# A convolution group ahead of the first head: which unit of work opens a kernel that TensorE bounds

## The chip, the cores and the metric

The kernel runs on one core of one Trainium2 chip. The metric is the device time of one execution in microseconds (us), where less is better. Three runs of the kernel before gave 903.43, 903.62 and 904.82 us; the median is 903.62. The chip's engines are named as follows: TensorE (PE in the profile) multiplies matrices and writes to PSUM; VectorE (DVE), ScalarE (ACT) and GpSimd (POOL) work element by element; SyncE (SP) issues the transfers.

## The reference

The reference computes one layer of a hybrid decoder on 2048 rows of 1024 columns, with 16 learned meta rows in front. All is float32. Cut to what matters:

```
hn = rms_norm(h, norm_g)                      # h: 16 meta rows, then x
proj = hn @ w_in                              # 1024 -> 8 * 512
cx, cb, cc, cg, q, k, v, rg = split(proj, 8)

conv_out = cb * conv3(cc * cx) * silu(cg)     # causal, 3 taps, per channel
q, k = rotary(q) * d**-0.5, rotary(k)         # 4 heads of 128
ret = group_norm(retention(q, k, v))          # chunks of 128 rows, a state per head
ret_out = ret * silu(rg)

h = h + concat(conv_out, ret_out) @ w_out
out = rms_norm(h, final_g)[16:]
```

The 512 channels of the convolution are four groups of 128, and the retention has four heads of 128. A group needs the four projections cc, cx, cg and cb; a head needs k, v, q and rg.

## The kernel before, in words

**Rounds and units.** The rows are worked in two rounds (`r`) of 1024 rows, each in two halves (`j`) of 512. A round consists of eight units: heads 0 to 3, then convolution groups 0 to 3. A last stage multiplies with `w_out`, pair by pair of row blocks.

**Quads.** Each unit has two quads. A quad multiplies two projections (`i`) by the two halves `j` of the round. A head's first quad gives K and V, its second Q and RG; a group's first gives CC and CX, its second CG and CB. For accuracy each float32 operand is split into a high and a low part (`split`, L99 on ScalarE for the cast and L111, or L103, on VectorE for the rest), and a product of blocks takes three matmuls for each of four slices of 128, so 12 matmuls of 128 by 512.

There are two kinds of quad. `quad` (matmuls at L208) needs seven products of blocks instead of eight, at the price of sums of blocks: `stationary` forms four sums of weight blocks on GpSimd (L108 and L111) and splits seven weight blocks, and `m` holds seven splits of x or of sums of its blocks. `quad_plain` (matmuls at L258) takes the blocks as they are, eight products. Round 0 opens with two plain quads, since the sums of x need time; round 1 opens with one, and the last stage with one.

**The opening of round 0.** While x is loaded and split, the two plain quads of the first unit run. Their weights are held in the tiles that later hold splits 2 and 3 of x (`FIRST_W`, `PLAIN_W`), and split 7 of x shares its tile with split 4 (`B12`). So those splits can only be made once a plain quad has passed: block sums are formed by `block_sums` (L172), splits 2 and 6 follow, and splits 3 and 4 are left to the function named `rest`, which is called after the unit's second quad through `between`. The normalisation of x is left out of the products: the factor of each row, `rr`, and its square, `rr2`, are made by `row_factors` (squares on ScalarE at L317, `rsqrt_mean`, and `spread`, which writes a diagonal to the tile `rot`, L281, multiplies it with ones, L288, and copies the result on ScalarE, L291 and L293), and multiplied in afterwards. The tile `rot` has one buffer, and the rotation of K and Q (`rotary`, L512 to L515) uses the same one.

**A head.** `take` copies or sums each result out of PSUM and rotates K and Q; RG is multiplied by `rr` (L556) and goes through Silu (L557). Then the meta rows give the first state (`meta_state`), and for each half K and V are transposed (L573, L578), states are updated (L588, L591), masked scores `pm` are formed (L601, L603) and applied (L611, L612), normalised (L617 to L628), transposed back (L635) and stored (`store_mixed`, L439). This follows the head's quads in program order, so it lies beside the quads of the next unit.

**A group.** In `conv_group` the first quad gives u = CC * CX * rr2. `meta_carry` gives the last two meta columns, `carry` copies them in front of u, `taps` applies the three taps (L452 on ScalarE, L454 twice on VectorE), and the second quad's results are multiplied in (L466, on VectorE and GpSimd).

**Beside the units.** After a unit's second quad `ahead` loads the next unit's raw weight blocks (L431) and, in round 0, multiplies them with the meta rows (`meta_products`, L392); only then may the block sums overwrite the raw blocks. After heads 1 to 3, two steps each of `later` prepare the block sums of the next round's x and of `w_out` in memory. After each group of round 0, three steps of `steps` make the row factors of round 1.

**What sets the order.** The program is written in the order above. A planner places the instructions of each engine from that order and from modelled times, when their inputs and a buffer are free; each engine then runs its own list strictly in order. The transfers all go through SyncE's queue. Buffers are shared by tag: `g` (16 tiles of a half row block, for x, u, K, V and others), `ra` (8 raw blocks), `tc` (4), `b` (2), and 4 banks of PSUM each for projections (`pj`) and for all else (`ms`).

The loop that the change touches:

```
        for h in range(NG):
            blocks = head(h, r, m, rot_t, f, blocks, lambda: ahead(r, h + 1), *((first, between) if h == 0 else ()))
            if h > 0:
                next(later, None)
                next(later, None)
        steps = row_factors(r + 1, factors[r + 1]) if r < NR - 1 else iter(())
        for g in range(NG):
            blocks = conv_group(g, r, m, f, blocks, lambda: ahead(r, NG + g + 1))
            for _ in range(3):
                next(steps, None)
```

Of the kernel before, what the change touches and what calls it, by code (L numbers as in the profile page):

```python
# [11 lines left out]
AF = mybir.ActivationFunctionType  # L12
# [7 lines left out]
NG = 4  # L20
EPS = 1e-6
HB = 512
# [9 lines left out]
BLOCK = ((0, 7), (1, 5))  # L32
FIRST_W, PLAIN_W, B12 = 2, 3, 4
SUMS = (3, 2, 4, 6)


def retention_constants():
# [31 lines left out]
def hybrid_trunk(ctx: ExitStack, tc: tile.TileContext, t, out: bass.AP, chunk_decay):  # L69
# [5 lines left out]
    nc = tc.nc  # L75
# [14 lines left out]
    def gen(name="g"):  # L90
        return sb.tile([P, HB + 16], F32, name=name, tag="g", bufs=GEN)[:, : 2 + HB]
# [21 lines left out]
    def load_raw(loads):  # L113
        tiles = []
        for load in loads:
            a = raw()
            load(a)
            tiles.append(a)
        return tiles

    def stationary(blocks):

        a11, a12, a21, a22 = blocks
        s1 = sb.tile([P, HB], F32, name="sa", tag="ra", bufs=RAW)

        def parts(src):
            hi = sb.tile([P, HB], F32R, name="wh", tag="wh", bufs=RING)
            lo = sb.tile([P, HB], F32R, name="wl", tag="wl", bufs=RING)
            split(hi, lo, src)
            return hi, lo  # L130

        w = [parts(a11), parts(a12)]
        add(nc.gpsimd, s1, a21, a22)
        sub(nc.gpsimd, a21, a11, a21)
        sub(nc.gpsimd, a11, s1, a11)
        sub(nc.gpsimd, a12, a12, a11)
        return w + [parts(a) for a in (a11, s1, a21, a12, a22)]
# [61 lines left out]
    def quad(w, m, take):  # L199


        def product(i, bank, first):
            (wh, wl) = w[i]
            for kt in range(KH):
                ks = slice(kt * P, (kt + 1) * P)
                mh, ml = m[i][kt]
                for n, (a, b) in enumerate(((wl, mh), (wh, ml), (wh, mh))):
                    nc.tensor.matmul(  # L208
                        bank, a[:, ks], b, start=first and kt == 0 and n == 0, stop=kt == KH - 1 and n == 2,
                        skip_group_check=not first,  # L210
                    )

        def copy(bank):
            c = sb.tile([P, HB], F32, name="tc", tag="tc", bufs=COPIES)
            nc.scalar.copy(out=c, in_=bank)  # L215
            return c

        xb = ps_proj()
        product(0, xb, True)
        c = copy(xb)  # L220
        yb = ps_proj()
        product(1, yb, True)
        take(0, 0, yb, c)
        product(2, xb, False)
        u2 = copy(xb)
        zb = ps_proj()
        product(3, zb, True)
        c = copy(zb)
        product(4, xb, False)
        take(1, 1, xb, c)  # L230
        product(5, zb, False)
        take(0, 1, zb, u2)
        product(6, xb, False)
        take(1, 0, xb, None)
# [195 lines left out]
    def w_loads(n):  # L430
        return [lambda a, i=i: nc.sync.dma_start(a, t["w_in"][n, i]) for i in range(4)]  # L431
# [18 lines left out]
    def taps(u, g):  # L450
        c = gen("c")[:, :HB]
        nc.scalar.mul(c, u[:, 2:], conv_w[:, g, 2:3])  # L452
        for tap in (1, 0):
            nc.vector.scalar_tensor_tensor(  # L454
                out=c, in0=u[:, tap : tap + HB], scalar=conv_w[:, g, tap : tap + 1], in1=c, op0=ALU.mult, op1=ALU.add
            )
        return c

    def conv_group(g, r, m, f, blocks, ahead):

        u = [gen("u") for _ in range(2)]
        rr, rr2 = ([a[:, j * HB : (j + 1) * HB] for j in range(2)] for a in f[:2])
        held = [None]

        def mul(eng, out, a, b):
            eng.tensor_tensor(out=out, in0=a, in1=b, op=ALU.mult)  # L466

        def take(i, j, pp, c):
            s = u[j][:, 2:]
            if c is None:  # L470
                mul(nc.vector, s, pp, s)
            elif i == 1:
                add(nc.vector, c, pp, c)
                held[0] = c
            else:
                add(nc.vector, s, pp, c)
                mul(nc.vector, s, s, rr2[j])
                if j == 1:
                    mul(nc.gpsimd, s, s, held[0])

        blocks, meta = blocks
        quad(stationary(blocks), m, take)
        if meta:
            meta_carry(g, meta)
        carry(u, g, r)
        cs = [taps(u[j], g) for j in range(2)]

        def take(i, j, pp, c):
            if i == 0:
                add(nc.vector, c, pp, c)  # L490
                mul(nc.vector, c, c, rr[j])
                nc.scalar.activation(c, c, AF.Silu)  # L492
                mul(nc.gpsimd, cs[j], cs[j], rr[j])
                mul(nc.gpsimd, cs[j], cs[j], c)
                return
            if c is not None:
                add(nc.vector, c, pp, c)
                pp = c
            mul(nc.vector, cs[j], pp, cs[j])

        n = 2 * (NG + g) + 1
        quad(stationary(load_raw(w_loads(n))), m, take)
        blocks = ahead()
        for j in range(2):
            store_mixed(r, j, g, cs[j])
        return blocks
# [205 lines left out]

    def ahead(r, n):

        if n == 2 * NG:
            return None
        blocks = load_raw(w_loads(2 * n))
        return blocks, meta_products(blocks) if r == 0 else None
# [4 lines left out]
    for r in range(NR):  # L723
        f = factors[r]
        rot_t = sb.tile([P, 2, BLK], F32, name="rot_t", tag="rot_t", bufs=1)
        p0 = NMETA + r * BLK

        def load_tables():
            nc.sync.dma_start(rot_t, t["rot"][:, :, p0 : p0 + BLK])

        if r == 0:
            w = [None] * 4
            loads = w_loads(0)

            def begin(half):
                for n in (half, 2 + half):
                    w[n] = plain_part(n, loads[n], FIRST_W)

            m, b = moving(
                load_x(r), gain_of, {(0, 0): lambda: begin(0), (0, KH - 1): lambda: begin(1), (0, KT - 1): normalise_meta}  # L740
            )
            first = [[p for a, p in w]]
            blocks = None, meta_products([a for a, p in w])
            first.append(plain_parts(w_loads(1)))
            load_tables()
            nc.sync.dma_start(cols, t["cols"])
            t3 = [a[:, i * HB : (i + 1) * HB] for a in (row_tile("t3") for _ in range(2)) for i in range(2)]
            t1 = [brief("t1") if n < BRIEF else sb.tile([P, HB], F32, name="t1", tag="tc", bufs=COPIES) for n in range(KH)]
            for kt in range(KH):
                b11, b21, b12, b22 = (b[n * KH + kt] for n in range(4))  # L750
                block_sums(b11, b12, b22, b21, t1[kt], t3[kt], gain_of(kt), gain_of(KH + kt), nc.gpsimd)
                parts(m, 2, kt, b22)
                parts(m, 6, kt, b21)
            for _ in row_factors(0, f):
                pass
            nc.sync.dma_start(causal, t["causal"])
            nc.sync.dma_start(conv_w, t["conv_w"])
            nc.sync.dma_start(ret_g, t["ret_norm_g"])

            def rest():  # L760
                for i, held in ((3, t1), (4, t3)):
                    for kt in range(KH):
                        parts(m, i, kt, held[kt])

            between = (lambda: None, rest)
            later = prepare(load_x(1), sums_x, gain_of)
        else:
            m, b = moving(load_x(r), gain_of)
            first = [plain_parts(w_loads(0))]
            load_tables()  # L770
            prepared(m, sums_x, (1, 3))
            between = (lambda: prepared(m, sums_x, (0, 2)),)
            blocks = None, None
            later = prepare(load_w_out, sums_w)
        for h in range(NG):
            blocks = head(h, r, m, rot_t, f, blocks, lambda: ahead(r, h + 1), *((first, between) if h == 0 else ()))
            if h > 0:
                next(later, None)
                next(later, None)
        steps = row_factors(r + 1, factors[r + 1]) if r < NR - 1 else iter(())  # L780
        for g in range(NG):
            blocks = conv_group(g, r, m, f, blocks, lambda: ahead(r, NG + g + 1))
            for _ in range(3):
                next(steps, None)

    m, b = moving(load_w_out)
    final_g = row_tile("final_g")
# [41 lines left out]
```

## Time and profile before

| | before |
|---|---|
| median of three runs | 903.62 us (903.43 to 904.82) |
| the profiled execution | 903.85 us, span 902.1 us |
| TensorE busy | 885.0 us, 98% of the span |
| VectorE busy | 714.6 us, 79% |
| ScalarE busy | 406.1 us, 45% |
| GpSimd busy | 398.9 us, 44% |
| mean granted clock of TensorE | 0.994 |

The span runs from the first to the last instruction of the profiled execution; 1.75 us of that execution lie around it. A row of a view of groups gives the source line, the engine, the operation, the tiles out<-in with their shapes, the count, then the busy time and the mean duration in ns, and then the idle time in front with what ended it. A row of a timeline gives start and duration in us. A row of windows gives the stretch, its length, the busy time of the engines PE, PEld (weight load), DVE, ACT and POOL with the number of instructions, then the granted clock of TensorE, the share of the transfer engines and GB/s. In a row of the waits, the last three numbers are the total in us, the number of waits and the longest one.

### The profile page before, as it was taken

To read this page: it belongs to the slowest core of one execution; us is meant where nothing else is said; L and a number is where in the kernel's file an instruction comes from. 1 tells how busy PE (TensorE), PEld (TensorE's weight loads), DVE (VectorE), ACT (ScalarE), POOL (GpSimd) and SP (SyncE) were. 2 spreads that over 40 slices of the span, in tenths; PEclk is the share of its full clock that TensorE was granted. 3 is DMA by queue.
4 is the path that set the end of the run, shared out by engine and by line. 5 is a ranking of instruction groups with operands and counts; after the bars stand their busy time and mean duration, and the time that the engine had idled before them with its cause. 6 is when DMAs were issued, how large, how long until landed. Compare 5 with 4: busy or idle time off the path is not lost.

```text
span 902.1 us, 12862 instructions
## 1 busy us (share of the span) xinstructions
PE 885.0 (98%) x4407; PEld 727.8 (81%) x4407; DVE 714.6 (79%) x1173; ACT 406.1 (45%) x815; POOL 398.9 (44%) x294
## 2 busy tenths in 40 slices
PE   8998999999999999999999999999999999999996
PEld 5787888888878777788888888888888878788885
DVE  6798888897686776899889899777667697866764
ACT  8771342424344443655333332433333465554553
POOL 0533132323355554461333323345546445777763
PEclk9998999999999999999999999999999999999999
DMA  9711352623234232744125262113231685555532
GB/s 333 239 40 38 104 195 59 205 82 107 79 103 127 78 108 78 253 180 141 38 73 203 73 236 68 50 56 90 57 88 48 210 280 178 162 186 152 182 111 93
DMA packets 76242, 116.94 MB, mean 130 GB/s; under 512 B 7632, under 2 KB 24336, under 8 KB 76176
## 3 DMA queue, kind: packets, MB, share of 16 engines
q1 hardware_dynamic: 76176, 116.11, 40.1%
q8 instruction: 35, 0.57, 0.3%
q14 instruction: 31, 0.25, 0.1%
HBM read 90.92 MB, written 25.17 MB: 129 GB/s over the span
## 4 chain that ended last, share of the span: by engine, by line
PE 83%; DVE 9%; DMA 3%; ACT 2%; issue 2%; POOL 1%; SPq 0%; POOLq 0%; DVEq 0%; ACTq 0%
PE pj L208 66%; PE pj L258 7%; DVE ml L111 2%; DVE wl L111 2%; PE ms L611 2%; PE ms L612 1%; PE ms L601 1%; PE ms L588 1%; PE ms L392 1%; DVE rot L513 1%; DMA ra<-in_w_in 1%; PE ms L635 1%; PE ms L573 1%; DVE rot L512 1%; PE ms L578 1%
## 5 line engine op out<-in xcount | busy, mean ns | idle before, releaser
L208 PE MATMUL pj<-mh,wl 128*128 128x512 f32 x1008 | 400.0, 397 | 1.0 <-ACT tc L215 0.8
L208 PE MATMUL pj<-ml,wh 128*128 128x512 f32 x1008 | 394.2, 391 | 1.1 <-DVE ml L111 1.1
L208 PE MATMUL pj<-mh,wh 128*128 128x512 f32 x1008 | 393.4, 390 | 0.0
L99 ACT CAST wh<-ra 128x512 fp32r<-128x512 f32 x216 | 133.8, 620 | 315.1 <-PE pj L208 272.4
L208 PEld LDWEIGHTS pj<-mh,wl 128*128 128x128 f32 x1008 | 189.6, 188 | 43.1 <-ACT tc L215 2.2
L208 PEld LDWEIGHTS pj<-ml,wh 128*128 128x128 f32 x1008 | 189.8, 188 | 39.6 <-DVE ml L111 1.9
L208 PEld LDWEIGHTS pj<-mh,wh 128*128 128x128 f32 x1008 | 189.6, 188 | 39.8
L111 DVE TENSOR_TENSOR wl<-ra,wh 128x512 fp32r<-128x512 f32 x216 | 192.4, 892 | 36.2 <-ACT wh L99 35.2
L111 POOL TENSOR_TENSOR ra<-ra 128x512 f32<-128x512 f32 x72 | 113.0, 1570 | 82.0 <-DVE qg L556 32.3
L108 POOL TENSOR_TENSOR sa<-ra 128x512 f32<-128x512 f32 x36 | 54.9, 1525 | 122.6 <-DVE wl L111 62.1
L111 POOL TENSOR_TENSOR ra<-sa,ra 128x512 f32<-128x512 f32 x36 | 52.2, 1450 | 98.3 <-DVE wl L111 98.0
L215 ACT COPY tc<-pj 128x512 f32<-128x512 f32 x108 | 62.6, 580 | 0.0
L258 PE MATMUL pj<-ml,mh 128*128 128x512 f32 x128 | 50.8, 396 | 0.1
L258 PE MATMUL pj<-mh,mh 128*128 128x512 f32 x128 | 50.2, 395 | 0.0
L258 PE MATMUL pj<-mh,ml 128*128 128x512 f32 x128 | 48.5, 396 | 1.5 <-DVE ml L111 1.5
L624 POOL TENSOR_TENSOR rp<-rs,neg_half 128x4 f32<-128x4 f32 x16 | 19.9, 1245 | 51.0 <-DVE rs L108 50.8
L466 POOL TENSOR_TENSOR c<-c,rr 128x512 f32<-128x512 f32 x16 | 30.0, 1874 | 24.0 <-DVE c L454 13.6
L108 DVE TENSOR_TENSOR tc<-pj,tc 128x512 f32<-128x512 f32 x32 | 22.0, 688 | 23.4 <-PE pj L208 23.4
L111 DVE TENSOR_TENSOR ml<-t,mh 128x512 fp32r<-128x512 f32 x40 | 36.6, 961 | 0.8 <-ACT mh L99 0.8
L99 ACT CAST wh<-sa 128x512 fp32r<-128x512 f32 x36 | 22.3, 620 | 32.7 <-PE pj L208 32.7
L665 DVE TENSOR_TENSOR yo<-pj,yo 128x512 f32<-128x512 f32 x32 | 22.0, 688 | 18.8 <-POOL yo L108 8.9
L466 POOL TENSOR_TENSOR c<-c,tc 128x512 f32<-128x512 f32 x16 | 27.3, 1706 | 19.0 <-ACT tc L492 17.6
(128 smaller groups left out, 1134.3 us busy)
## 6 DMA issues: line engine op xcount, KB each, us to landing
ra<-in_w_in SPq DMA_DIRECT2D x128, 256.0 KB, 2.7
x<-in_xT SPq DMA_DIRECT2D x48, 256.0 KB, 5.1
w<-in_w_out SPq DMA_DIRECT2D x32, 256.0 KB, 5.0
ra<-mixed SPq DMA_DIRECT2D x32, 256.0 KB, 2.7
yo<-in_x SPq DMA_DIRECT2D x32, 256.0 KB, 4.4
ra<-in_x SPq DMA_DIRECT2D x16, 256.0 KB, 3.7
mixed<-qg SPq DMA_DIRECT2D x16, 256.0 KB, 2.3
sums_x<-x SPq DMA_DIRECT2D x16, 256.0 KB, 2.4
```

The source lines that it names most:

```text
L99: nc.scalar.copy(out=hi, in_=src)
L108: eng.tensor_tensor(out=out, in0=a, in1=b, op=ALU.add)
L111: eng.tensor_tensor(out=out, in0=a, in1=b, op=ALU.subtract)
L208: nc.tensor.matmul(bank, a[:, ks], b, start=first and kt == 0 and n == 0, stop=kt == KH - 1 and n == 2, skip_group_check=not first,)
L215: nc.scalar.copy(out=c, in_=bank)
L258: nc.tensor.matmul(banks[i], a[:, ks], b, start=half + kt + n == 0, stop=half == 1 and kt == KH - 1 and n == 2,)
L392: nc.tensor.matmul(four[i], meta_s[:, i % 2 * KH + kt, :], blocks[i][:, kt * P : (kt + 1) * P], start=kt == 0, stop=kt == KH - 1,)
L466: eng.tensor_tensor(out=out, in0=a, in1=b, op=ALU.mult)
L512: nc.vector.tensor_tensor(out=rot[:h, :w], in0=a[h:], in1=table[h:, 1, :], op=ALU.mult)
L611: nc.tensor.matmul(o[:, cs], pm[:, cs], vt[j][:, cs], start=True, stop=False)
L624: nc.gpsimd.tensor_tensor(out=rp, in0=rs, in1=neg_half.rearrange("p (c a) -> p c a", a=1), op=ALU.pow)
L665: last[0] = nc.vector.tensor_tensor(out=y, in0=pp, in1=y, op=ALU.add)
```

## The change

The order of the units is written down in a table, and round 0 runs group 0 first, then heads 0 to 3, then groups 1 to 3. Round 1 keeps its order. The two plain quads of round 0 go to group 0: the first weights loaded are those of CC and CX, the next those of CG and CB. `conv_group` gets a plain form of its two quads: in the first, CC is copied out of PSUM by ScalarE and CX multiplied onto it by VectorE, and the products with `rr2` follow when the quad is done; in the second, all four results are copied by ScalarE and multiplied afterwards. Head 0 takes the seven-product quads. Because one group now stands ahead of the heads, the steps that make the row factors of round 1 are taken four at a time after groups 1 to 3.

```
+UNITS = (4, 0, 1, 2, 3, 5, 6, 7), (0, 1, 2, 3, 4, 5, 6, 7)
...
-    def conv_group(g, r, m, f, blocks, ahead):
+    def conv_group(g, r, m, f, blocks, ahead, first=(), between=()):
+        between = iter(between)
...
+        def take_plain(i, j, pp, c):
+            s = u[j][:, 2:]
+            if i == 0:
+                nc.scalar.copy(out=s, in_=pp)
+            else:
+                mul(nc.vector, s, pp, s)
+
         blocks, meta = blocks
-        quad(stationary(blocks), m, take)
+        if len(first) > 0:
+            quad_plain(first[0], m, take_plain)
+        else:
+            quad(stationary(blocks), m, take)
+        next(between, lambda: None)()
+        if len(first) > 0:
+            for j in range(2):
+                mul(nc.vector, u[j][:, 2:], u[j][:, 2:], rr2[j])
         if meta:
             meta_carry(g, meta)
         carry(u, g, r)
         cs = [taps(u[j], g) for j in range(2)]
+
+        def take_plain(i, j, pp, c):
+            c = gen("cb")[:, :HB]
+            nc.scalar.copy(out=c, in_=pp)
+            if i == 0:
+                mul(nc.vector, c, c, rr[j])
+                nc.scalar.activation(c, c, AF.Silu)
+                mul(nc.gpsimd, cs[j], cs[j], rr[j])
+            mul(nc.vector, cs[j], cs[j], c)
...
-        quad(stationary(load_raw(w_loads(n))), m, take)
+        if len(first) > 1:
+            quad_plain(first[1], m, take_plain)
+        else:
+            quad(stationary(load_raw(w_loads(n))), m, take)
+        next(between, lambda: None)()
         blocks = ahead()
...
-            loads = w_loads(0)
+            loads = w_loads(2 * NG)
...
-            first.append(plain_parts(w_loads(1)))
+            first.append(plain_parts(w_loads(2 * NG + 1)))
...
-            def rest():
+            def late_parts():
...
-            between = (lambda: None, rest)
+            between = (lambda: None, late_parts)
...
         steps = row_factors(r + 1, factors[r + 1]) if r < NR - 1 else iter(())
-        for g in range(NG):
-            blocks = conv_group(g, r, m, f, blocks, lambda: ahead(r, NG + g + 1))
-            for _ in range(3):
-                next(steps, None)
+        units = UNITS[r]
+        for n, unit in enumerate(units):
+            following = units[n + 1] if n + 1 < len(units) else None
+            rest = lambda: ahead(r, following)
+            special = (first, between) if n == 0 else ()
+            if unit < NG:
+                blocks = head(unit, r, m, rot_t, f, blocks, rest, *special)
+                if unit > 0:
+                    next(later, None)
+                    next(later, None)
+            else:
+                blocks = conv_group(unit - NG, r, m, f, blocks, rest, *special)
+                if n > 0:
+                    for _ in range(4 - r):
+                        next(steps, None)
```

More of the change, by code (lines that the diff above doesn't have):

```diff
@@ L713, in ahead @@
     def ahead(r, n):
-        if n == 2 * NG:
+        if n is None:
             return None
@@ L774, in hybrid_trunk @@
             later = prepare(load_w_out, sums_w)
[L775 to L779, printed above, removed]
-        steps = row_factors(r + 1, factors[r + 1]) if r < NR - 1 else iter(())
-        for g in range(NG):
-            blocks = conv_group(g, r, m, f, blocks, lambda: ahead(r, NG + g + 1))
-            for _ in range(3):
-                next(steps, None)
+        steps = row_factors(r + 1, factors[r + 1]) if r < NR - 1 else iter(())
+        units = UNITS[r]
[13 more added lines that the diff above has]
+                        next(steps, None)
     m, b = moving(load_w_out)
```

## The prediction

> **What bounds the kernel now.** I read the page first. TensorE is busy for nearly the whole span, so the kernel can only get shorter where TensorE stands still or runs at a lower clock.
>
> ```profile
> span 902.1 us, 12862 instructions
> PE 885.0 (98%) x4407; PEld 727.8 (81%) x4407; DVE 714.6 (79%) x1173; ACT 406.1 (45%) x815; POOL 398.9 (44%) x294
> ```
>
> The waits of TensorE come second. One wait holds most of what can be won: a matmul of a head's retention waits for the masked scores pm, which VectorE writes. The next row shows how small the others are.
>
> ```profile
> PE ms L611 <- DVE pm L603: 3.7, 1, 3.7
> PE pj L208 <- ACT tc L215: 0.8, 2, 0.7
> ```
>
> Third come the windows around it. The last column but two is the granted clock.
>
> ```profile
> 65.00:76.06 11.06, 11.06 (x60) 9.27 (x60) 10.88 (x18) 3.93 (x9) 3.19 (x2) 1.00 0.19 49
> 76.06:79.81 3.75, 0.00 (x1) 0.00 (x1) 3.70 (x8) 0.62 (x1) 0.00 (x0) 0.85 0.25 70
> 79.81:85.52 5.71, 5.71 (x22) 5.23 (x22) 3.47 (x14) 0.00 (x0) 2.01 (x3) 0.50 0.12 46
> 78.60:78.80 0.20, 0.00 (x0) 0.80 0.00 0
> ```
>
> In the hole VectorE is busy for 3.70 of 3.75 us, so VectorE is the bound there. The clock falls to half inside the slice 78.60 to 78.80, some 2.7 us into the hole, and stays there for 5.7 us of work after it. The timeline of TensorE prices this, with two rows of the later chain for the same retention matmuls at full clock.
>
> ```profile
> 75.22 0.39 PE L208 MATMUL pj<-mh,wl 128*128 128x512 f32 x1
> 75.67 0.39 PE L208 MATMUL pj<-mh,wh 128*128 128x512 f32 x1
> 79.81 0.79 PE L611 MATMUL ms<-kv,pm 128*128 128x128 f32 x2 [3.75 <-DVE pm L603]
> 83.24 0.77 PE L208 MATMUL pj<-mh,wl 128*128 128x512 f32 x1
> 85.52 0.42 PE L208 MATMUL pj<-mh,wh 128*128 128x512 f32 x1
> 439.05 0.22 PE ms L611 x2
> 440.83 8.18 PE pj L208 x36
> ```
>
> Sixteen small matmuls took 83.24 - 79.81 = 3.43 us, where the later sixteen took 440.83 - 439.05 = 1.78: 1.65 lost. The five large steps from 83.24 to 85.52 took 2.28 us; at full clock (75.22 to 75.67 is two steps, 0.225 each) they take 1.13: 1.15 lost. Hole and clock together are 3.75 + 2.8 = 6.55, say 6.5 us.
>
> Why is VectorE late there? The chain of waits from 48 us on is nearly all VectorE, and its work is head 0's rotation.
>
> ```profile
> 54.06 0.69 DVE rot L512
> 76.68 0.70 DVE rot L513
> 79.09 0.67 DVE pm L603
> ```
>
> In the code the scratch tile rot has one buffer, and the row factors take it ahead of head 0. So no rotation can start until the second diag (L281) has been used, and the K, Q and retention work of head 0 piles up behind 54 us, beside the weight splits of head 1.
>
> **The change, part by part.** *Matrix work.* A plain quad has 8 products of 12 matmuls, the other kind 7. Conv group 0 takes the two plain quads and head 0 takes the seven-product kind, so the count stands: no term.
>
> *What leaves the opening.* Head 0's 16 rotation steps on VectorE, between 0.677 and 1.183 us each, so 10.8 to 18.9 us, and its transposes, state updates and score matmuls move behind head 0's own later quads, where they lie beside head 1, as those of heads 1 to 3 do now without a wait.
>
> ```profile
> L513 DVE TENSOR_TENSOR rot<-kv,rot_t 64x512 f32<-64x512 f32 x16 | 18.9, 1183 | 0.2
> L108 DVE TENSOR_TENSOR qg<-qg,rot 128x512 f32<-128x512 f32 x16 | 10.8, 677 | 0.1
> L466 DVE TENSOR_TENSOR u<-u,rr 128x512 f32<-128x512 f32 x16 | 16.4, 1027 | 0.0
> L454 DVE SCALAR_TENSOR_TENSOR c<-u,conv_w,c 128x512 f32<-128x512 f32 x32 | 22.1, 742 | 0.4 <-POOL u L445 0.3
> L466 DVE TENSOR_TENSOR tc<-tc,rr 128x512 f32<-128x512 f32 x16 | 14.2, 887 | 0.0
> L466 DVE TENSOR_TENSOR c<-tc,c 128x512 f32<-128x512 f32 x8 | 6.6, 820 | 0.0
> L466 POOL TENSOR_TENSOR c<-c,rr 128x512 f32<-128x512 f32 x16 | 30.0, 1874 | 24.0 <-DVE c L454 13.6 <-DVE c L466 10.5
> ```
>
> *What comes in.* After the row factors VectorE gets 2 products with rr2 (2 x 1.03), 4 taps (4 x 0.74), 2 of gate by rr (2 x 0.89) and 4 into the result (4 x 0.82): 10.1 us; the two out of PSUM come earlier, in the first quad, where VectorE has room. GpSimd gets two products of 1.87 us and small column copies, ScalarE the copies that the head also had. So by 79 us VectorE has 0.7 to 8.8 us less to do, and no retention matmul stands in TensorE's queue there. I take the old hole as gone: -6.5 us.
>
> *What is late next.* Now nothing of head 0 separates the first products of the second unit. Its third product needs weights that are made in a chain: meta products on TensorE (which read the raw blocks), two block sums on GpSimd, a cast on ScalarE, a split on VectorE.
>
> ```profile
> 53.64 0.60 ACT L293 ACTIVATE rr<-ms 128x512 f32<-128x512 f32 x1
> 57.46 0.66 PE L573 MATMUL ms<-ident,kv 128*128 128x128 f32 x4
> 58.31 0.48 PE L208 MATMUL pj<-mh,wl 128*128 128x512 f32 x1
> 63.88 1.05 PE L588 MATMUL ms<-kv,kd 128*128 128x128 f32 x8
> 65.82 0.48 PE L208 MATMUL pj<-mh,wl 128*128 128x512 f32 x1
> 57.66 1.71 POOL L111 TENSOR_TENSOR ra<-ra 128x512 f32<-128x512 f32 x1 [8.90 <-PE ms L392]
> 59.45 1.62 POOL L111 TENSOR_TENSOR ra<-sa,ra 128x512 f32<-128x512 f32 x1
> 61.10 0.62 ACT L99 CAST wh<-ra 128x512 fp32r<-128x512 f32 x1 [0.23 <-POOL ra L111]
> 64.85 0.67 DVE L111 TENSOR_TENSOR wl<-ra,wh 128x512 fp32r<-128x512 f32 x1
> 50.35 3.69 DVE L111 TENSOR_TENSOR ml<-t,mh 128x512 fp32r<-128x512 f32 x6
> 59.95 3.37 DVE L111 TENSOR_TENSOR ml<-t,mh 128x512 fp32r<-128x512 f32 x2
> ```
>
> Before, the split was done at 65.52 and the third product began at 65.82. But TensorE spent 58.31 - 57.46 = 0.85 and 65.82 - 63.88 = 1.94 us of that on head 0's transposes and states. Without them it asks for the product at 65.82 - 2.79 = 63.0 us. The weights then come between 61.72 + 0.67 = 62.4 us (chain alone, no queue on VectorE) and about 71 (worked out in rival 3). I take 65.5, as measured: VectorE's queue from 48 to 65 us loses 8 rotation steps (5.4 to 9.5 us by the rows above) and gains the 10.1, of which the last two (1.6) can lie behind the split; that is near enough to no change. The stall S is then 65.5 - 63.0 = 2.5 us, shorter than the 2.7 us after which the clock fell above. Later products need one split in 2.7 us (12 x 0.225), which VectorE can do.
>
> [...]
>
> *Edits at nothing.* The row-factor steps of round 1 go four to a group instead of three; the last of them (spread of the second half, with two ScalarE copies) now comes after group 3.
>
> ```profile
> L291 ACT COPY rr<-ms 128x512 f32<-128x512 f32 x4 | 2.4, 589 | 0.7 <-PE ms L288 0.7
> 345.00:366.00 21.00, 21.00 (x93) 17.10 (x92) 13.36 (x18) 6.74 (x12) 8.67 (x8) 1.00 0.25 76
> ```
>
> Its inputs are ready during group 3, where ScalarE is busy 6.74 of 21 us: cost 0; if that cover is gone, 2 x 0.59 = 1.2 us in front of round 1. It can't gain. The x loads for it, the head's rot_m load and the conv stores move in SP's queue; weight loads behind them are issued a quad ahead, so 0. meta_carry for meta_state is one transpose for one matmul: 0.
>
> **Sum.** The profiled execution took 903.85 us (span 902.1 and 1.75 around it), 0.23 above the median of 903.62. 903.85 - 6.5 + 2.5 = 899.85 us.
>
> **The rivals.** All share 897.35 + S, plus 2.8 when S passes 2.7.
>
> 1. *No new stall.* GpSimd's chain runs ahead of the conv work and VectorE takes the split at once (62.4, before 63.0): S = 0, 897.35 us. For it: VectorE has less to do in all. Against: conv steps and the held-back splits stand ahead in program order.
>
> 2. *The hole only moves.* S between 2.7 and 5.4 with the clock gone: 897.35 + 2.7 + 2.8 = 902.85 to 905.55, no change that can be told (0.2%, 1.8 us, is what a measurement of this kernel tells). For it: VectorE is slow while GpSimd works: six splits took 3.69 us alone (0.62 each), two took 3.37 beside the block sums. The change adds two GpSimd products of 1.87 us at this place. [...]
>
> 3. *Slower: GpSimd's queue.* If cs1 by rr stands ahead of the block sums in GpSimd's queue, the weights wait for the whole conv chain: rr2 at 54.24, product 1.03, ScalarE tap 0.74 (priced as a VectorE tap), two taps 1.48, GpSimd 1.87, block sums 1.71 + 1.62, cast 0.62, split 0.67 = 64.0 us with nothing queued; with the first half's conv work (1.03 + 1.48 + 0.89 = 3.4) and the two late splits (3.37) ahead on VectorE, 70.8. Then S = 7.8 and the time 897.35 + 7.8 + 2.8 = 907.95. It decides from weights later than 63.0 + 5.5 = 68.5 us on. Against: TensorE's meta products end at 57.5, before cs1 is likely to be ready.
>
> **Chances.** Forecast 0.42 (range 897.9 to 900.1), no stall 0.16, hole moved 0.20, GpSimd's queue 0.22. Faster 0.42 + 0.16 = 0.58, same 0.20, slower 0.22. The range reaches from rival 1, less the 0.2 us of the median, to 906.9, that is weights at 69.7 us; about half of rival 3 and a little below are left out.
>
> **What would show it.** Right: no wait of L611 for pm near 80 us; the waits of TensorE name a wl split or ScalarE's copy at some 63 to 66 us, under 2.7 us long; granted clock 1.00 from 10 to 890 us; no rot step before head 0's first product. Wrong: a slice at 0.50 between 55 and 100 us, GpSimd's c<-c,rr just ahead of its ra<-ra at 57 to 60, a wait at the turn to round 1 above the 0.7 quoted, or waits in heads 1 to 3.

## The result, and the profile after

The changed kernel took 906.71 us (median of seven runs, 905.01 to 907.68) against 903.43 us for the kernel before beside it: 1.0035 times as long, with a 95% interval of 1.0022 to 1.0049. It is slower by some 3 us, where the prediction forecast 899.85. The profiled execution took 906.71 us too, so its trace stands for the median. One of the eight executions of a later kernel, the one with the whole tail put off, took 1485.31 us at a mean clock of 0.557, and that kernel's figures below are those of the other seven, 898.85 us at the median instead of 898.98.

The page of the kernel after, its first lines and its busy times:

```profile
span 904.9 us, 12864 instructions
PE 882.2 (97%) x4407; PEld 726.5 (80%) x4407; DVE 717.7 (79%) x1176; ACT 407.7 (45%) x816; POOL 392.2 (43%) x291
```

The waits of TensorE after, the largest first (total, number, longest):

```profile
PE pj L210 <- DVE wl L113: 7.0, 2, 6.5
...
PE pj L210 <- ACT wh L101: 0.6, 1, 0.6
```

The wait of a retention matmul for pm, 3.75 us long before, is gone. In its place a product of head 0 (L210 is now the line of the seven-product matmuls) waits 6.5 us for the low part of a weight block, wl. The windows around it, with the columns of the prediction's windows:

```profile
60.00:64.00 4.00, 3.96 (x18) 2.93 (x16) 4.00 (x4) 3.38 (x9) 2.64 (x3) 1.00 0.00 0
64.00:68.00 4.00, 0.00 (x0) 0.00 (x0) 4.00 (x6) 1.66 (x3) 2.94 (x2) 0.86 0.00 0
68.00:72.00 4.00, 1.58 (x4) 1.29 (x5) 4.00 (x7) 0.00 (x0) 0.00 (x0) 0.50 0.47 134
72.00:76.00 4.00, 4.00 (x16) 3.18 (x15) 3.68 (x5) 0.95 (x2) 2.31 (x2) 0.79 0.45 129
```

From 60 to 72 us VectorE has no free moment. GpSimd and ScalarE are idle in the second half of the hole. Here is TensorE's timeline at its two edges:

```profile
63.57 0.39 PE L210 MATMUL pj<-mh,wh 128*128 128x512 f32 x1
70.42 0.80 PE L210 MATMUL pj<-mh,wl 128*128 128x512 f32 x1 [6.46 <-DVE wl L113]
73.58 0.46 PE L210 MATMUL pj<-ml,wh 128*128 128x512 f32 x1
```

This is the third product, and it is asked for at 70.42 - 6.46 = 63.96 us; the prediction said 63.0. Seven large steps took 73.58 - 70.42 = 3.16 us; at 0.225 each they take 1.58. So the half clock costs 1.6 us here, and hole and clock cost 8.0 us, more than the 6.5 us that went. By the shares in the windows the clock was at half from 66.9 to 73.7 us.

What VectorE did in that time, from its timeline:

```profile
56.81 2.72 DVE L456 SCALAR_TENSOR_TENSOR c<-u,conv_w,c 128x512 f32<-128x512 f32 x2
59.46 1.78 DVE L470 TENSOR_TENSOR cb<-cb,rr 128x512 f32<-128x512 f32 x1
61.16 0.74 DVE L456 SCALAR_TENSOR_TENSOR c<-u,conv_w,c 128x512 f32<-128x512 f32 x1
61.82 0.68 DVE L470 TENSOR_TENSOR cb<-cb,rr 128x512 f32<-128x512 f32 x1
62.42 3.46 DVE L113 TENSOR_TENSOR ml<-t,mh 128x512 fp32r<-128x512 f32 x2
65.81 1.35 DVE L110 TENSOR_TENSOR mk<-mk 16x128 f32<-16x128 f32 x1
67.09 0.67 DVE L470 TENSOR_TENSOR c<-c,cb 128x512 f32<-128x512 f32 x1
67.69 0.27 DVE L110 TENSOR_TENSOR mk<-mk 16x128 f32<-16x128 f32 x1
67.89 1.88 DVE L470 TENSOR_TENSOR c<-c,cb 128x512 f32<-128x512 f32 x3
69.70 0.67 DVE L113 TENSOR_TENSOR wl<-ra,wh 128x512 fp32r<-128x512 f32 x1
```

The split that TensorE waits for is the last row. Ahead of it stand the taps, the products of the gate by rr (cb), the two late splits of x, the meta sums of head 0 (mk) and all four products into the group's result. Of these only the splits of x are needed soon. When could the split of the weights have started? The chain through GpSimd and ScalarE shows it:

```profile
62.05 1.63 POOL L470 TENSOR_TENSOR c<-c,rr 128x512 f32<-128x512 f32 x1 [1.36 <-ACT cb L511]
63.63 1.71 POOL L113 TENSOR_TENSOR ra<-sa,ra 128x512 f32<-128x512 f32 x1
65.37 0.62 ACT L101 CAST wh<-ra 128x512 fp32r<-128x512 f32 x1 [1.59 <-POOL ra L113]
```

The group's second product c by rr stands ahead of the second block sum on GpSimd, as rival 3 had it (the first ran at 57.71 us, ahead of the sum before). Even so the cast was done at 65.37 + 0.62 = 66.0. A split right after it would have been done at 66.7, and the hole 2.7 us long. The other 3.7 us, until 70.4, are VectorE's own list.

A smaller difference lies at the opening. The small matmuls of ones by state, which stand at the same place in TensorE's list in both kernels, start 0.3 us later. (TensorE's busy time in the first 10 us, 6.65 us against 7.43 before, overstates this, as the last section shows.) First the row of the kernel before, then that of the kernel after:

```profile
15.46 0.55 PE L376 MATMUL ms<-ones,state 128*16 128x1 f32 x16
```

```profile
15.77 0.55 PE L378 MATMUL ms<-ones,state 128*16 128x1 f32 x16
```

### The profile page after: what moved, and what is told of

It is laid out like the page before. It is cut to its first block, busy times and chain, and to the rows that moved or that the text cites. A ratio compares the mean times of both kernels' runs of the same rounds, so it can differ in the third digit from the quotient of the medians.

```text
span 904.9 us, 12864 instructions
## 1 busy us (share of the span) xinstructions
PE 882.2 (97%) x4407; PEld 726.5 (80%) x4407; DVE 717.7 (79%) x1176; ACT 407.7 (45%) x816; POOL 392.2 (43%) x291
## 4 chain that ended last, share of the span: by engine, by line
PE 81%; DVE 8%; DMA 3%; ACT 3%; issue 2%; POOL 1%; SPq 0%; POOLq 0%; DVEq 0%; ACTq 0%
PE pj L210 67%; PE pj L260 5%; DVE ml L113 2%; DVE wl L113 2%; PE ms L642 1%; PE ms L619 1%; PE ms L643 1%; PE ms L632 1%; DMA ra<-in_x 1%; DMA x<-in_xT 1%; PE ms L394 1%; PE ms L604 1%; PE ms L609 1%; PE ms L666 1%; ACT mh L104 1%
## 5 line engine op out<-in xcount | busy, mean ns | idle before, releaser
L210 PE MATMUL pj<-mh,wl 128*128 128x512 f32 x1008 | 400.5, 397 | 9.6 <-DVE wl L113 7.0
L210 PE MATMUL pj<-ml,wh 128*128 128x512 f32 x1008 | 394.7, 392 | 1.1 <-DVE ml L113 1.1
L210 PE MATMUL pj<-mh,wh 128*128 128x512 f32 x1008 | 394.1, 391 | 0.0
L210 PEld LDWEIGHTS pj<-mh,wl 128*128 128x128 f32 x1008 | 189.9, 188 | 52.2 <-DVE wl L113 7.4
L210 PEld LDWEIGHTS pj<-mh,wh 128*128 128x128 f32 x1008 | 189.7, 188 | 39.8
L210 PEld LDWEIGHTS pj<-ml,wh 128*128 128x128 f32 x1008 | 190.1, 189 | 39.1 <-DVE ml L113 1.4
L659 DVE TENSOR_SCALAR pm<-ms,mv,rp 128x128 f32<-128x128 f32 x64 | 21.9, 405 | 15.8 <-POOL rp L655 15.8
L701 POOL TENSOR_TENSOR z<-yo,final_g 128x512 f32<-128x512 f32 x16 | 26.2, 1635 | 18.5 <-DVE yo L696 18.5
```

Source lines behind the costliest of these rows:

```text
L210: nc.tensor.matmul(bank, a[:, ks], b, start=first and kt == 0 and n == 0, stop=kt == KH - 1 and n == 2, skip_group_check=not first,)
L659: nc.vector.tensor_scalar(out=y[:, cs], in0=o[:, cs], scalar1=mv[:, c, 0:1], scalar2=rp[:, c, :], op0=ALU.subtract, op1=ALU.mult,)
L701: nc.gpsimd.tensor_tensor(out=ys[i][j], in0=y, in1=final_g[:, j * HB : (j + 1) * HB], op=ALU.mult)
```

## The experiments

Each kernel ran in five rounds beside the kernel before. Lines in diffs are cut to what is edited.

**The group's last work put off.** The changed kernel, with the second half of the group's work (gate by rr, Silu, c by rr, the four products) set behind head 0's fourth weight split on VectorE and behind its last block sum on GpSimd.

```
-            if i == 0:
-                mul(nc.vector, c, c, rr[j])
...
+            held_back.append((i, j, c))
+
+        def finish():
+            with tc.issue_after(marks[3].ins), tc.issue_after(marks["sums"].ins):
+                for i, j, c in held_back:
...
```

> The changed kernel, with the group's last work (gate by rr, Silu, cs by rr, the four products into the result, and the stores) written after head 0's first quad and queued on VectorE behind the split of the fourth product's weights, on GpSimd behind the last block sum. Nothing is left out. Theory 1 (the 6.5 us hole is the third product waiting for a split that stands behind the group's products in VectorE's queue): the hole shrinks to about 1 us (split done near 65 instead of 70.4, TensorE asks at 63.9), no half clock, and the time falls by 5.5 + 1.4 to about 899.8 us, below the kernel before. Rival (the conv work has to be done before head 0 can go on, so the stall only moves to a later product or a later unit): within 2 us of the changed kernel, 905 to 907, with a new wait between 66 and 110 us.

It took 902.18 us (901.06 to 903.69), 0.9989 of the kernel before (0.9979 to 0.9999): about 4.5 us less than the changed kernel, and level with the kernel before by the 0.2% bound. (The profiled execution took 903.51, among the longest; it lost the clock once more near 771 us, as the last section shows.) Its VectorE and TensorE timelines:

```profile
65.52 0.67 DVE L112 TENSOR_TENSOR wl<-ra,wh 128x512 fp32r<-128x512 f32 x1
```

```profile
66.34 0.47 PE L212 MATMUL pj<-mh,wl 128*128 128x512 f32 x1 [1.82 <-DVE wl L112]
```

The hole fell from 6.46 to 1.82 us. What was expected for the hole was near; what was not expected is that a gap of 1.82 us still cost the clock. The windows of TensorE (busy, then granted clock) show it at half speed from 67.46 to 70.88 us, worked out from the shares in the first and the last row:

```profile
67.00:67.50 0.50, 0.50 (x4) 0.96 0.18 66
67.50:68.00 0.50, 0.50 (x3) 0.50 0.35 135
70.50:71.00 0.50, 0.50 (x3) 0.62 0.00 0
```

**GpSimd relieved.** The changed kernel, with c by rr of the opening group on VectorE.

```
-                mul(nc.gpsimd, cs[j], cs[j], rr[j])
+                mul(nc.vector, cs[j], cs[j], rr[j])
```

> The changed kernel, with the two products cs by rr of the opening group on VectorE instead of GpSimd. Nothing is left out. GpSimd's block sums then follow the meta products at once, so the raw weights of the third product are ready near 61.2 us instead of 65.3. If GpSimd's queue sets the hole (rival 3 as predicted): the hole is gone, split done near 63, about 898.8 us. If VectorE's queue sets it: ten of the group's products still stand ahead of the split, which is done near 67.5 to 68, the hole is about 4 us, and the time 903.5 to 905.

It took 904.21 us (903.72 to 906.36), 1.0015 of before (1.0004 to 1.0026). GpSimd's block sums now follow one another, and the one that the third product needs is done at 59.86 + 1.63 = 61.49 us instead of 65.34. But ScalarE casts it only at 65.56, since a Silu (L511) that waits for VectorE's gate product stands ahead of the cast. The rows of GpSimd, ScalarE, VectorE and TensorE:

```profile
59.86 1.63 POOL L113 TENSOR_TENSOR ra<-sa,ra 128x512 f32<-128x512 f32 x1
65.03 0.63 ACT L511 ACTIVATE cb<-cb 128x512 f32<-128x512 f32 x1 [0.63 <-DVE cb L470]
65.56 0.60 ACT L101 CAST wh<-ra 128x512 fp32r<-128x512 f32 x1
66.12 0.68 DVE L113 TENSOR_TENSOR ml<-t,mh 128x512 fp32r<-128x512 f32 x1
67.13 1.28 DVE L470 TENSOR_TENSOR c<-c,cb 128x512 f32<-128x512 f32 x2
68.33 0.67 DVE L113 TENSOR_TENSOR wl<-ra,wh 128x512 fp32r<-128x512 f32 x1
69.15 0.77 PE L210 MATMUL pj<-mh,wl 128*128 128x512 f32 x1 [4.25 <-DVE wl L113]
```

So the hole shrank by 2.2 us (6.46 to 4.25), but only 1.4 of them are an earlier split (68.33 instead of 69.70); the rest is that TensorE asks later, at 69.15 - 4.25 = 64.90 us. The cast was no sooner than in the changed kernel (66.2 us against 66.0), so GpSimd's queue did not set the hole. VectorE came to the split sooner although it had the two products c by rr in addition. Two of the four products into the result now stand behind the split, and the two late splits of x took 0.68 us each while GpSimd was idle, where they had taken 3.46 together beside its work.

**The old pile-up taken away in the kernel before.** Head 0 first, as before; the diagonals of the row factors get a tile of their own, so the rotations of K needn't wait for them (the tiles `b` give the space).

```
-        diag = sb.tile([P, HB], F32, name="rot", tag="rot", bufs=1)...
+        diag = sb.tile([P, HB], F32, name="diag", tag="diag", bufs=1)...
```

> The kernel before, with a tile of its own for the diagonal of the row factors (the two brief tiles are cut from 640 to 544 columns, of which 512 are used, to make room). Nothing is left out. Theory (the hole of 3.75 us near 76 us comes from head 0's rotations piling up behind 54 us, since they share one buffer with the diagonal): the rotations of K start before 40 us, the wait for pm near 80 us and the half clock go, and the time falls by up to 6.5 us to 897 to 900. Rival (VectorE has too much to do in the opening in whatever order): the hole stays or moves, within 1.5 us of the kernel before.

It took 905.75 us (903.45 to 908.11), 1.0028 of before (1.0013 to 1.0043): slower. The rotations of K ran early, 38 us and before, but they took VectorE's time from the splits of x, which run later, and all of Q's rotations (49.62 to 67.4 us) now stand ahead of the weight split, where they stood behind it before (from 65.55 us). The TensorE timeline has the same kind of hole as the changed kernel, and a second one much later:

```profile
68.13 0.77 PE L208 MATMUL pj<-mh,wl 128*128 128x512 f32 x1 [4.33 <-DVE wl L111]
134.34 0.49 PE L611 MATMUL ms<-kv,pm 128*128 128x128 f32 x2 [1.82 <-DVE pm L603]
```

After the second, the windows of TensorE show half clock again:

```profile
136.00:137.00 1.00, 1.00 (x7) 0.50 0.80 225
```

Freeing the late tile only moved the hole; VectorE's list up to the weight split is too long here as well.

**The row-factor steps alone.** The kernel before, with four steps after groups 1 to 3 instead of three after each group.

```
-            for _ in range(3):
-                next(steps, None)
+            if g > 0:
+                for _ in range(4):
+                    next(steps, None)
```

> The kernel before, with only the row-factor steps of round 1 changed: none after group 0, four each after groups 1 to 3. Nothing is left out. If that edit costs nothing, as predicted: within 0.5 us of the kernel before. If it is what makes the small waits between 300 and 345 us and at the turn to round 1 in the changed kernel: slower by 0.6 to 1.5 us, with a wait of TensorE for a cast or a copy of ScalarE there.

It took 901.77 us (900.44 to 904.86), 0.9986 of before (0.9973 to 0.9999), inside the 0.2% that can't be told from no change. That is 1.4 us below the kernel before beside it, more than the 0.5 us either way that was expected, but the edit costs nothing, as predicted. Round 1 begins between 350 and 400 us, and TensorE is busy for 49.32 of these 50 us in the kernel before and for 49.43 in this one, at a clock of 1.00 in both.

**The whole tail put off.** As in the first experiment, and also the products with rr2, the column copies, the taps, and head 0's meta state.

```
+        def middle_part():
+            if len(first) > 0:
+                for j in range(2):
+                    mul(nc.vector, u[j][:, 2:], u[j][:, 2:], rr2[j])
+            carry(u, g, r)
+            cs.extend(taps(u[j], g) for j in range(2))
...
+            with tc.issue_after(marks[3].ins), tc.issue_after(marks["sums"].ins):
+                middle_part()
...
+            with tc.issue_after(held_at.pop()) if held_at else nullcontext():
+                meta_state(h, blocks[1])
```

> As e1_behind, but the whole tail of the opening group (the products of u with rr2, the column copies, the taps, the gate and the four products) and head 0's two meta sums stand behind the split of the fourth product's weights on VectorE and behind the block sums on GpSimd. Nothing is left out. Theory 1 (VectorE's queue ahead of the split is the whole hole, and a short hole still costs a stretch of half clock): the split is done near 63.5 us, TensorE asks near 64, no wait over 0.3 us there and no slice at 0.50; e1_behind's remaining 1.8 us and its 3.4 us at half clock (1.7 us lost) go too, so about 3.5 us below e1_behind, 898 to 899.5 us. Rival (the work put off fills VectorE later and a wait comes back between 70 and 110 us): 900.5 to 902.5, with that wait in the list.

It took 898.85 us (897.75 to 900.68), 0.9956 of before (0.9941 to 0.9971): faster than both kernels. VectorE's timeline has the split 8.5 us earlier than in the changed kernel, now after a wait of 1.84 us for the cast, and the group's products behind it; the largest wait of TensorE for a split is 0.9 us:

```profile
61.18 1.23 DVE L112 TENSOR_TENSOR wl<-ra,wh 128x512 fp32r<-128x512 f32 x1 [1.84 <-ACT wh L101]
62.94 1.28 DVE L472 TENSOR_TENSOR u<-u,rr 128x512 f32<-128x512 f32 x2
```

```profile
PE pj L212 <- DVE wl L112: 2.1, 3, 0.9
```

**The first weights' place in memory.** The changed kernel, with the weight blocks stored in the order in which they are read, group 0's first.

```
+        n = n - 2 * NG if n in (2 * NG, 2 * NG + 1) else n + 2 if n < 2 * NG else n
...
+    tiles = tiles[2 * NG : 2 * NG + 2] + tiles[: 2 * NG] + tiles[2 * NG + 2 :]
```

> The changed kernel, with the blocks of w_in stored in the order in which this kernel reads them, so that the first weights loaded lie at the front of the array, as in the kernel before. No instruction changes but the addresses of the weight loads. In the three kernels profiled with the group first, the fourth cast of x began at 7.8 to 8.4 us; in the three with head 0 first at 6.8 to 7.6. If the place of the weights in memory makes the first loads slower: TensorE is busy 0.5 to 1.0 us more before 20 us, and the time is that much shorter. If the difference is chance: no change there, within 0.5 us of the changed kernel.

The opening came forward: the small matmuls of ones by state start at 14.88 us, against 15.77 in the changed kernel and 15.46 before. But it took 907.57 us (906.26 to 908.39), 1.0048 of before (1.0033 to 1.0064), no less than the changed kernel's 1.0035 (1.0022 to 1.0049). TensorE's timeline at the opening and at the hole, and two windows around the hole:

```profile
14.88 0.55 PE L378 MATMUL ms<-ones,state 128*16 128x1 f32 x16
69.78 0.80 PE L210 MATMUL pj<-mh,wl 128*128 128x512 f32 x1 [6.51 <-DVE wl L113]
```

```profile
64.00:68.00 4.00, 0.00 (x0) 0.00 (x0) 4.00 (x6) 1.66 (x3) 2.29 (x2) 0.67 0.00 0
72.00:76.00 4.00, 4.00 (x11) 3.12 (x10) 2.69 (x4) 0.65 (x2) 2.88 (x2) 0.55 0.37 92
```

The hole is as long as before, but it begins (63.27 us) and ends (69.78) 0.6 to 0.7 us sooner than in the changed kernel. That gain went to the clock. By the shares it is at half from 65.4 to 75.6 us (all of 68 to 72), 10.2 us instead of 6.8; of these 5.8 us instead of 3.3 are work behind the hole, which loses 2.9 us instead of 1.6. More clock is lost late in the kernel: the mean from 700 to 896 us is 0.99, where the changed kernel has 1.00 from 700 us to the end of its span. This is the profiled execution, at 908.39 us the longest of the six; the others have no trace.

**Both together.** The whole tail put off, and the same places in memory.

> e6_all_behind and the stored order of e7_layout together. Nothing is left out. If both theories hold: 897 to 898.5 us, 0.5 to 0.7% below the kernel before. If the place in memory does nothing: as e6_all_behind.

It took 898.44 us (897.53 to 900.26), 0.9952 of before (0.9936 to 0.9968). That is 0.4 us less than with the tail put off alone, which the intervals can't tell apart. The small matmuls of ones by state start at 15.07 us, against 15.41 there. Whether this gain at the opening can be kept to the end stays open.

**Head 0 first, with its tail put off.** Is the order of the units worth anything, if queueing decides? The kernel before, with head 0's scores and all that follows them written behind head 1's first quad.

```
+        def retain():
+            for j in range(2):
+                sc = ps_misc()
...
+        if r == 0 and h == 0:
+            return blocks, retain
+        retain()
...
+            special = (first, between) if h == 0 else ((), retain) if r == 0 and h == 1 else ()
```

> The kernel before (head 0 first) with one edit: the second part of head 0 (scores, pm, the retention matmuls, the norm, the store) is written behind the first quad of head 1 instead of ahead of it, so that TensorE takes its first retention matmul some 25 large steps (5.6 us) later, and VectorE has that much more time for the rotations. Theory 1 (what costs is only that the opening unit's tail stands too early in the in-order lists; which unit opens is worth nothing): the wait for pm at 76 to 80 us and the half clock behind it go, nothing comes in their place, and the time is 903.4 - 6.5 = 897 us, between 896.5 and 898.5, level with the group-first kernel whose tail was put off (898.98). Rival 2 (VectorE has too much to do here, and head first can't be mended by order alone, as when the rotations were let start early): a wait of TensorE of 2 us or more for pm or a wl split somewhere between 60 and 95 us, with a slice at half clock, and 901 to 905 us. In between, a wait under 1.5 us without half clock: 898.5 to 900.

It took 905.23 us (902.57 to 906.68), 1.0025 of before (1.001 to 1.004): slower, near the rival's side, though its waits are a little shorter than the rival's 2 us. The hole near 80 us became two, each of them with the clock gone behind it. Its TensorE timeline, and its windows of TensorE after each of them:

```profile
81.14 0.50 PE L208 MATMUL pj<-mh,wl 128*128 128x512 f32 x1 [1.80 <-DVE kv L108]
132.21 0.49 PE L612 MATMUL ms<-kv,pm 128*128 128x128 f32 x2 [1.93 <-DVE pm L604]
```

```profile
82.00:82.50 0.50, 0.50 (x3) 0.69 0.20 74
82.50:83.00 0.50, 0.50 (x3) 0.50 0.00 0
85.50:86.00 0.50, 0.50 (x5) 0.90 0.00 0
...
134.00:134.50 0.50, 0.50 (x4) 0.50 0.91 168
```

The holes take 3.73 us together, as long as the one before (3.75), and a half-clock stretch follows each.

**Group first with its whole tail put off, again, on the chip of the last one.**

> The group-first kernel with the whole tail of the opening group behind head 0's first split and block sums, once more, on the same chip as the head-first kernel with its tail put off. It took 898.98 us. Theory 1 (the order of the units is worth nothing by itself): within 2 us of the head-first one with its tail put off. If the group-first order were worth something by itself, it is 3 us or more below that one; if it costs something, as its slower opening (0.8 us) would have it, up to 2 us above.

It took 898.22 us (897.45 to 899.3), 0.9955 of before (0.9942 to 0.9968), 7.0 us below the head-first kernel beside it. So the two ways of putting work off are not level. That the order of the units itself is worth something is not shown by this: in the head-first kernel head 0's rotations, transposes and states were left where they stood, its first hole waits for a rotation (kv, L108), and a head-first kernel with these put off too was not run. The windows from 60 to 70 us show VectorE (the third pair of numbers) full in the head-first kernel and with room in this one. First the head-first kernel, then this one:

```profile
60.00:70.00 10.00, 9.89 (x52) 8.34 (x51) 9.89 (x15) 5.93 (x16) 3.17 (x3) 1.00 0.10 28
```

```profile
60.00:70.00 10.00, 9.45 (x43) 7.52 (x42) 8.57 (x12) 5.68 (x10) 6.61 (x7) 1.00 0.08 26
```

## Why the prediction was wrong

**Right: the old hole, and its price.** No retention matmul waits near 80 us, and with the new hole nearly gone, the kernel with its whole tail put off took 898.17 and 898.49 us in its profiled executions, 0.8 and 1.1 us above the prediction's floor of 897.35. Its three waits for a split (2.1 us in all, the longest 0.9) are of that order. The price of 6.5 us is that of the profiled execution; others of the same kernel lost less or more to the clock, as the last section shows.

**Right: the edits at nothing.** The row-factor steps cost nothing by themselves. And the new wait is at the place that the prediction named, the third product of head 0, asked for at 63.96 us (63.0 predicted).

**The step that failed: S, the time of the weights.** The prediction took the split to be done at 65.5 us, as before, since it held the work that VectorE loses and the work that it gains over 48 to 65 us to be nearly equal. The split was done at 69.70 + 0.67 = 70.4. The bounds held (62.4 to about 71), but the balance didn't, and S came out as 6.46 us instead of 2.5. The list ahead of the split began 1.15 us later (its first six splits of x at 51.50 us instead of 50.35), and from their end to the weight split it took 14.5 us instead of 10.8. Two things made it longer:

- The order. "The last two products can lie behind the split" was an assumption, and all four stood ahead. The planner put the whole tail of the group ahead of it on VectorE, which worked through it from 55.55 us (the first tap) on and came to the split at 69.70. With the tail's second half behind it the split began at 65.52 us, with the whole tail at 61.18, and the wait fell from 6.46 to 1.82 us and then to under 1.
- The pace. The group's rows ahead of the split add up to 9.9 us, near the 10.1 of the prediction, but rows beside GpSimd's work are slow (two splits took 3.46 us beside it here, and 0.68 each with GpSimd relieved). Measured against 0.68 us for a product or a split, 0.74 for a tap and 0.27 for a meta sum, this costs an estimated 5.5 us in the list shown above, and 3.0 in the kernel before. What the pace alone is worth was not run.

**Rival 3: near in time, right in half its reason.** It gave weights at 70.8, a hole of 7.8 and 907.95 us. The measured hole is 6.46, and the profiled time 906.71. It had c by rr ahead of the block sums on GpSimd and the group's work ahead of the split on VectorE, and both were so: the prediction's argument against it (that c by rr would not be ready before the block sums) failed, as one of the two stood ahead of these sums, at 57.71 us, and one between them, from 62.05 to 63.68. But it put the cause in GpSimd's queue, and the run with GpSimd relieved shows that the split comes only 1.4 us sooner when the block sum is done 3.9 us sooner.

**The clock.** The sum's condition, no clock loss under 2.7 us, was read from where the clock fell inside a long hole. Gaps of 1.80 to 1.93 us lost the clock in the experiments, so the forecast S of 2.5 could have cost clock as well. In the changed kernel the loss was 1.6 us, not the 2.8 of the formula, as TensorE stood still for about half of the 6.8 us at half clock.

**What is left of the sum.** 897.35 + 6.46 + 1.6 = 905.4, and the profiled execution took 906.71. The opening, 0.3 us later, and a new wait of 0.6 us for ScalarE's cast, which also stands in the kernel with its tail put off, are part of the rest; neither was tested by itself to the end of the kernel.

**What the prediction said would show it.** It named a slice at 0.50 between 55 and 100 us and c by rr just ahead of a block sum as signs that it was wrong; both are in the trace. That the mended version is faster than both kernels says that the mechanism of the forecast, a hole exchanged for a smaller one, is there, but only if the list of VectorE is ordered for it.

## What to carry to other kernels

Where a tail of work is moved beside the start of the next unit, don't compare the sum of work on the busy engine: list, in its order, what will stand ahead of the one instruction that the bound engine waits for. If it is urgent and the planner doesn't know, put the rest behind it by an explicit order (898.2 to 898.9 us instead of 906.7 here). Making the cause of a hole earlier (905.75 us) or later (905.23) only moved the hole here, since the engine that feeds TensorE stayed full.

## What the runs showed of the hardware

**Half clock behind gaps of 1.80 to 1.93 us.** The half-clock stretch after the gap of 1.82 us (the last work put off) lasted from 67.46 to 70.88, 3.42 us; after that of 1.80 us (the head-first kernel with its tail put off) it lasted from 82.19 to 85.60, 3.41 us, both worked out from the shares in the rows above. Each began after TensorE had resumed (at 66.34 and 81.14 us), 1.0 to 1.1 us later. The gaps of 1.82 us in the head-first kernel with its own tile and of 1.93 us in the one with its tail put off were followed by half clock too (0.50 from 136 to 137 us and from 134 to 134.5). The longest waits for a split in the two runs with the group's whole tail put off, 0.9 and 1.0 us, cost no clock (1.00 from 60 to 105 us and from 60 to 150).

**Two short gaps in the last stage, with the clock lost and with it kept.** In the second quad of the last stage TensorE stands still twice within 2.2 us, for some 0.57 and 1.12 us, and this pair comes out both ways. First the kernel with the group's last work put off, then the changed kernel, each with a window of TensorE behind the pair (length, busy, clock):

```profile
770.53 0.74 PE L212 MATMUL pj<-ml,wh 128*128 128x512 f32 x1 [1.12 <-DVE ml L112]
771.00:774.00 3.00, 3.00 (x8) 0.50 0.00 1
```

```profile
774.98 0.50 PE L210 MATMUL pj<-ml,wh 128*128 128x512 f32 x1 [1.11 <-DVE ml L113]
776.00:779.00 3.00, 3.00 (x15) 1.00 0.10 20
```

In the first TensorE runs at half clock from 771 to 774 us, in the second at full clock from 776 to 779. Eight profiles have the second wait, 1.1 us for ml. The mean clock from 700 to 901 us is 0.98 with the last work put off and with the row-factor steps alone, 0.99 with GpSimd relieved, and 1.00 in the head-first kernel with its own tile; with the stored weights it is 0.99 from 700 to 896 us. (The means to 901 us hold TensorE's idle end too, which alone gives the kernel before its 0.99: 1.00 from 700 to 895 us, 0.71 from 895 to 902.) The changed kernel, the head-first one with its tail put off and the second run of the whole tail put off have 1.00 from 700 to 850 us. What decides whether such a pair costs the clock was not shown.

Executions of one kernel differ in the clock. In 69 executions of the kernel before beside the experiments the mean granted clock lies between 0.990 (two of them, 905.51 and 906.22 us) and 0.998 or 0.999 (four, 899.0 to 900.3 us). The kernels with the whole tail put off took 897.5 to 899.1 us at 0.998 or 0.999. The lowest times at such a clock are 1.5 us apart (899.0 and 897.5), while their medians lie 4.3 to 4.8 us below the kernel before beside them: so a good part of their gain is, by an estimate from these times, clock that is not lost. Where the clock fell in executions without a trace is not known.

**VectorE's pace beside GpSimd.** Two splits took 3.46 us in the changed kernel between 62.42 and 65.88, where GpSimd worked; with GpSimd relieved and idle they took 0.68 each. The whole trace of the changed kernel says the same. Of VectorE's products, sums and splits of two blocks of 128x512 (rows of one instruction, none of their inputs in PSUM), 247 ran with no GpSimd work on such blocks beside them, and none took more than 0.69 us. Of 144 that ran beside such work 57% took more than 1 us, up to 1.84. Why the others beside it were not slow is open.

**The place of the first weights in memory.** With the weights stored in the order in which they are read, the small matmuls of ones by state start at 14.88 and 15.07 us in two profiles. In the five other profiles with the group first they start between 15.41 and 16.39, in the four with head 0 first between 14.69 and 15.67. So the stored order may bring the opening forward, by less than the spread of one opening, and this is not settled. TensorE's busy time in the first 10 us can't tell it. It is 7.43 us in the kernel before and 6.65 in the changed one, but the same work took longer in the first: nine matmuls on the tile warm 4.02 us, against 3.66, and from the first large step to the second 0.59 us (6.21 to 6.80), against 0.33 (6.50 to 6.83).
